# Five seven-product pairs in the second round of a feed-forward network, and later transposes into attention, on one Trainium2 core

## The chip, the core and the metric

The kernel runs on one core of one Trainium2 chip. A core has a matrix engine (TensorE, PE in the profile), a vector engine (VectorE, DVE), a scalar engine (ScalarE, ACT), GpSimd (POOL) and a queue engine (SyncE, SP) that issues most transfers. Each engine works through its own list of instructions in order and waits for semaphores of the others. PE reads its operands from SBUF and writes sums into eight banks of PSUM of 128 x 512 float32; DVE and ACT read them out.

The metric is device time in microseconds (us). A comparison of two kernels on this program can tell about 0.2% (2.6 us) from no change.

## The reference

One sequence of 512 tokens of width 1024 goes through two layers: a Mamba-2 mixer and a feed-forward network, then latent attention and a second feed-forward network, each with a residual and a layer norm behind it. What the change touches is this part:

```python
def conv_ffn(h, up, conv_w, conv_b, down):
    u = causal_depthwise_conv(h @ up, conv_w, conv_b)     # 1024 -> 2 x 2816, 3 taps
    g, val = jnp.split(u, 2, axis=-1)
    return (jax.nn.silu(g) * val) @ down                  # 2816 -> 1024
...
        h = layer_norm(DN_ALPHA * h + mix, ln_mix_g[i], ln_mix_b[i])
        ff = conv_ffn(h, ffn_up[i], ffn_conv_w[i], ffn_conv_b[i], ffn_down[i])
        h = layer_norm(DN_ALPHA * h + ff, ln_ffn_g[i], ln_ffn_b[i])
```

Behind the first feed-forward network, attention begins with two products on `h`: `h @ q_down` (384 columns) and `h @ kv_down_proj` (320 columns).

## The kernel before

Every float32 operand is split into a high part (the value rounded to PE's format) and the low remainder, and a product is three matmuls: high x high, high x low, low x high. Weights pass through `WStream`: SP loads a tile of 128 x 1024 into `wst`, ACT casts it to `wh` (line 96), DVE subtracts to get `wl` (line 97). Six `wh`/`wl` pairs exist, so ACT and DVE can prepare the weights of an item only when an earlier one has been used up.

A feed-forward network has 22 channel tiles (`HT`) of 128 hidden channels. For each one PE makes 48 matmuls (`mm_a`, line 159; gate and value), and `conv3_silu_gate` makes the convolution and the gating on ACT and DVE. The hidden tiles go into the down projection in two ways:

- In pairs (`down_pairs`). A pair of channel tiles, two halves of the tokens and two halves of the output columns form a product of 2 x 2 blocks, which is made with seven block products in place of eight. Each of the seven (a11, s1, s2, s4, s3, a12, a22) is made for two token tiles, by three matmuls of 512 columns for each pair; its operands are sums made on DVE (`pair_operands`), and the sums of weights are made by DMA accumulation and by DVE. The results go into the residual `h` from three sets of banks X, Y, Z (`add`, line 387).
- Directly (`piece`). For token tile i and column half hf, one bank sums the remaining channel tiles; `add_mix` (line 185) adds it into `h` with the row sum for the layer norm.

There are two rounds: round r makes its channel tiles, then its pairs. `RP0` and `RP1` give the numbers of pairs for the first and the second layer: `((2, 2, 1), (2, 1, 1))` is five pairs, in weight items of two, two and one, in the first round, and four pairs in the second. So ten channel tiles go into the first round, eight into pairs of the second, and four are left for the direct way. All hidden operands lie in 18 tiles (`gt`), given out in turn.

The end of the first network is where most of the argument lies. For each token tile i in order: two pieces, two `add_mix`, then the layer norm: `ln_mean` (line 189, DVE), `ln_squares` (194, ACT), `ln_var` (203 and 204, two operations on 128 x 1 that GpSimd makes, the second a power), `ln_a` twice (210, DVE, from `h` and the parameters `lng` into `xn`), `ln_b` twice (215, DVE, into `h`). Then `transpose_h(i)`: PE transposes the eight blocks of the tile (line 274, four into each of two banks), and ACT and DVE split each bank into the halves high and low of `ht` (277, 278). Attention's first step `down(i)` (in `mla`) needs `ht` of tile i: 48 matmuls in 16 entries on six weight items `dw`; behind it a normalisation makes `ctok`, which `down_t(i)` transposes. Before the change, tiles 0 and 1 are transposed within the network, tile 2 behind `down(0)` and tile 3 behind `down(1)`.

A scheduler decides the order on PE, DVE, ACT and GpSimd from the order in which the code issues; only SP's order is written by hand.

Of the kernel before, what the change touches and what calls it, by code (L numbers as in the profile page):

```python
# [20 lines left out]
NT = SEQ // P  # L21
DM = 1024
KT = DM // P
HID = 2816
HT = HID // P
# [259 lines left out]

RP0 = ((2, 2, 1), (2, 1, 1))
RP1 = ((2, 2, 1), (2, 1, 1))


def rounds(rp):
    r0 = 2 * sum(rp[0])
    return r0, r0 + 2 * sum(rp[1])


def ffn_items(up, down, rp):

    it = []
    R0, R1 = rounds(rp)
    dv = down.rearrange("(k p) n -> p k n", p=P)
    for r, ks in enumerate((range(R0), range(R0, HT))):
        for c in ks:
            it.append((up[c], 1024))
            it.append((up[c + HT], 1024))

        for odd, hf, kinds in ((0, 0, "r"), (0, 1, "a"), (1, 1, "+="), (0, 0, "-"), (1, 0, None), (1, 0, "a")):
            j = ks[0]  # L310
            for p, n in enumerate(rp[r]):
                b = dv[:, j:j + 2 * n, hf * 512:(hf + 1) * 512].rearrange("p (k e) n -> p k e n", e=2)[:, :, odd, :]
                it += [(b, n * 512, kind, p) for kind in kinds or (None,)]
                j += 2 * n
    for hf in range(2):
        for j in range(R1, HT, 2):
            it.append((dv[:, j:j + 2, hf * 512:(hf + 1) * 512], 1024))
    return it
# [39 lines left out]
    split(k, s34, v)  # L358


def down_pairs(k, ws, n, prs, parts, first, between):

    nc = k.nc
    X, Y, Z = ([k.bank() for _ in range(2)] for _ in range(3))
    ni = len(parts)
    at = [sum(parts[:p]) for p in range(ni + 1)]
    new = {(i, hf) for i in range(NT) for hf in range(2)} if first else set()  # L370

    def product(bs, op, p, i, start, stop):
        wh, wl = ws.get(i, 3)
        ps = prs[at[p]:at[p + 1]]
        for t in range(2):
            for q, pr in enumerate(ps):
                x, c0 = pr[op]
                sl = slice(q * 512, (q + 1) * 512)
                k.mm_b(bs[t], x, slice(c0 + t * P, c0 + (t + 1) * P), wh[:, sl], wl[:, sl],
                       start and p == 0 and q == 0, stop and p == ni - 1 and q == len(ps) - 1)  # L380
        ws.retire(i)

    def add(bs, row, hf, sign):
        for t in range(2):
            i = 2 * row + t
            hs = k.h[:, i, hf * 512:(hf + 1) * 512]
            last = nc.vector.scalar_tensor_tensor(hs, hs, ALPHA if (i, hf) in new else 1.0, bs[t], op0=ALU.mult,  # L387
                                                  op1=ALU.add if sign > 0 else ALU.subtract)
            new.discard((i, hf))
        return last  # L390

    def ahead(n, ins):

        with k.tc.issue_after(ins.ins):
            ws.ahead(n)

    for p in range(ni):
        product(X, "a11", p, n + p, True, True)
    n += ni
    ahead(n, add(X, 0, 0, 1))  # L400
    for p in range(ni):
        product(Y, "s1", p, n + p, True, True)
    n += ni
    ahead(n, add(Y, 1, 1, 1))
    between()
    for p in range(ni):
        product(X, "s2", p, n + 2 * p, False, True)
        product(Y, "s4", p, n + 2 * p + 1, False, True)
    n += 2 * ni
    add(X, 0, 1, -1)  # L410
    ahead(n, add(Y, 0, 1, 1))
    for bs, op, s0, out in ((X, "s3", False, (1, 1, -1)), (Z, "a12", True, (0, 0, 1)), (X, "a22", False, (1, 0, 1))):
        for p in range(ni):
            product(bs, op, p, n + p, s0, True)
        n += ni
        ahead(n, add(bs, *out))
    return n


def ffn(k, ws, base, cwp, gb, rp, la=2, out=None, mid=None):  # L420

    nc, tc = k.nc, k.tc
    R0, R1 = rounds(rp)
    with ExitStack() as c:
        pool = lambda n, b: c.enter_context(tc.tile_pool(name=n, bufs=b))
        pools = {"gt": pool("gt", 18), "fw": pool("fw", 7), "rs": pool("rs", 1), "cw": pool("cw", 1)}
        k.junk = (pools["fw"], "acc")
        cw = pools["cw"].tile([P, 2 * HT, 4], F32, name="cw")
        nc.sync.dma_start(cw, cwp)
        n = base  # L430
# [3 lines left out]
        rs = k.lnp.tile([P, 2, DM], F32, name="rs", tag="lngb")  # L434
        ws.sums = [rs[:, 0], rs[:, 1], pools["rs"].tile([P, 512], F32, name="rs2")]
        new_gt = lambda: pools["gt"].tile([P, 2, SEQ], F32R, name="gt")
# [8 lines left out]
        for r in range(2):  # L445
            gts, prs = [], []

            half = [new_gt().rearrange("p x (e t) -> p e x t", e=2) for _ in range((sum(rp[r]) + 1) // 2)]
            even = []

            def finish(ci, bg, bv):
                if ci >= R1:
                    gts.append(new_gt())
                    conv3_silu_gate(k, pools, bg, bv, cw, ci, gts[-1])
                    return
                av = conv3_silu_gate(k, pools, bg, bv, cw, ci, None)
                if ci % 2 == 0:
                    even.append(av)
                    return
                j = len(prs)  # L460
                a11, a2, s12, s34 = half[j // 2][:, j % 2], new_gt(), new_gt(), new_gt()
                pair_operands(k, pools, even.pop(), av, a11, a2, s12, s34)
                prs.append({"a11": (a11, 0), "a12": (a2, 0), "a22": (a2, 256), "s1": (s12, 0), "s2": (s12, 256),
                            "s3": (s34, 0), "s4": (s34, 256)})

            c0 = r * R0
            if k.pend:

                nh = 2 + len(k.pend)
                bs = [k.bank() for _ in range(4)]  # L470
                wv = lambda i, la=None: [x.rearrange("p (k m) -> p k m", k=KT) for x in ws.get(n + i, la)]
                for i in range(nh - 1):
                    k.mm_a(bs[i][:, :256], wv(i, nh - 2 - i), k.ht, slice(0, 256))
                k.flush()
                with tc.issue_after(k.ln_end.ins), tc.issue_after(k.ln_sq.ins):
                    ws.ahead(n + nh - 1, 0)
                    ws.ahead(n + 5, 0)
                k.mm_a(bs[nh - 1][:, :256], wv(nh - 1, 0), k.ht, slice(0, 256))
                for i in range(4):
                    c = 256 if i < nh else 0  # L480
                    k.mm_a(bs[i][:, c:], wv(i, 0), k.ht, slice(c, 512))
                    ws.retire(n + i)
                    if i % 2:
                        ws.ahead(n + i + 1)
                        finish(c0 + i // 2, bs[i - 1], bs[i])
                n += 4
                c0 += 2
            for ci in range(c0, HT if r else R0):
                bg, bv = k.bank(), k.bank()
                ws.ahead(n + 1)  # L490
                for b, i in ((bg, n), (bv, n + 1)):
                    w = [x.rearrange("p (k m) -> p k m", k=KT) for x in ws.get(i)]
                    k.mm_a(b, w, k.ht, slice(0, 512))
                    ws.retire(i)
                n += 2
                ws.ahead(n)
                finish(ci, bg, bv)
            if mid and not r:
                mid()
            n = down_pairs(k, ws, n, prs, rp[r], not r, norm_params if r else lambda: None)  # L500
        if out is None:
            k.new_ht()

# [21 lines left out]
        for i in range(NT):  # L525
            last = i == NT - 1
            b = k.bank()
# [14 lines left out]
            b = k.bank()  # L542
# [1 line left out]
            if last:  # L544
                ws.ahead(n + 2 * nw, la)
            k.add_mix(i, 1, b, 1.0, True)
            if out is None and i >= 2:
                k.transpose_h(i - 2)
            xn[i] = row("xn")
            k.ln_stats(i)  # L550
            if out is None:
# [7 lines left out]
        n += 2 * nw  # L559
    ws.nst = 3  # L560
    if out is None:
        k.pend = [lambda: k.transpose_h(NT - 2), lambda: k.transpose_h(NT - 1)]
    return n

NH, HD, NG, HPG, NS = 32, 64, 8, 4, 128
# [6 lines left out]

LAG = [15, 15, 7.6, 5, 7.6, 13]
DRAM = bass.MemoryType.DRAM


def ssd_items(xbc, zdt, zw, ow):
# [540 lines left out]
def mla(k, ws, base, ngp, gb):  # L1118
    nc, tc = k.nc, k.tc
    with ExitStack() as cx:  # L1120
# [16 lines left out]
        n = [base]  # L1137
        tok = {}

        def down(i):  # L1140
            bq, bk = k.bank(), k.bank()
            ts = slice(i * P, (i + 1) * P)
            plan = []
# [6 lines left out]
                plan.append((j, bq[:, :QR], 5 + 2 * (j - 4), QR, QR))  # L1150
            seen = set()
            for c, (j, o, kk, off, w) in enumerate(plan):
                wh, wl = ws.get(n[0] + j)
                last = o.shape[1] == QR and kk == 7 or o.shape[1] != QR and kk == 7
                k.mm_b(o, ht[kk], ts, wh[:, off:off + w], wl[:, off:off + w], kk == 0, last)
                if i == NT - 1 and (c == len(plan) - 1 or plan[c + 1][0] != j):
                    ws.retire(n[0] + j)
# [54 lines left out]
            rope(k, qr[:, i].rearrange("p (h d) -> p h d", h=AH), b.rearrange("p (h d) -> p h d", h=AH), i, AH, tmp, nc.gpsimd)  # L1212

        for i in range(NT):
            down(i)
            if k.pend:
                k.pend.pop(0)()
            if i:
                down_t(i - 1)
        H = {}  # L1220
# [231 lines left out]
```

## Time and profile before

| | |
|---|---|
| time, median of 3 runs (range) | 1312.17 us (1312.11 to 1312.66) |
| the profiled execution's own time | 1312.25 us |
| its span, first to last instruction | 1310.5 us |
| PE busy | 1300.4 us, 99% of the span |
| DVE busy | 1014.7 us, 77% |
| ACT busy | 635.0 us, 48% |
| POOL busy | 93.6 us, 7% |
| share of PE in the chain that ended last | 94% |

The first network's second round of pairs and its direct pieces lie between about 674 and 772 us of the span, and attention's first step begins at 772.60. The 1.75 us between the span and the time lie outside the instructions and are taken as fixed.

### The profile page before, as it was taken

Reading aid. Unit: us, or ns where it says so; the run is one execution under the profiler, and the core shown is the slowest. Engines: PE = TensorE matmul, PEld = TensorE weight load, DVE = VectorE, ACT = ScalarE, POOL = GpSimd, SP = SyncE. Lnnn points to the kernel's source line nnn. Section 1 sums busy time; section 2 is a strip of 40 time slices with the busy share of each in tenths; the row PEclk is TensorE's granted clock in tenths of the full one; section 3 lists DMA queues with packets and bytes.
Section 4 is the critical chain, followed back from the end, with each engine's and each line's share of the span. In section 5 each row is a group of like instructions: output and inputs, shape, how many; then the busy total and the mean of one; then the engine's idle time right before and its main releaser. Section 6 shows DMA issues by size and latency. Waiting matters only on the chain.

```text
span 1310.5 us, 17403 instructions
## 1 busy us (share of the span) xinstructions
PE 1300.4 (99%) x6666; PEld 1098.0 (84%) x6666; DVE 1014.7 (77%) x1581; ACT 635.0 (48%) x1029; POOL 93.6 (7%) x96
## 2 busy tenths in 40 slices
PE   9999999999999999999999999999999999999997
PEld 8888888888888988888888899888898888888886
DVE  7688898787798868866776876998587686667587
ACT  5765555456353644444443434665254444444341
POOL 0111011011011001100000012000100010000000
PEclk9999999999999999999999999999999999999999
DMA  8423314313420533352322721320143227322251
GB/s 297 179 113 113 121 41 145 129 44 135 167 73 1 179 129 82 71 204 98 125 65 33 247 88 61 104 90 33 35 149 136 77 35 215 129 97 105 41 161 65
DMA packets 49780, 144.59 MB, mean 110 GB/s; under 512 B 5313, under 2 KB 6337, under 8 KB 48417
## 3 DMA queue, kind: packets, MB, share of 16 engines
q1 hardware_dynamic: 44480, 133.57, 29.0%
q0 software_dynamic: 5072, 9.77, 4.4%
q8 instruction: 52, 0.85, 0.3%
q14 instruction: 32, 0.25, 0.1%
q10 hardware_dynamic: 144, 0.15, 0.0%
HBM read 141.30 MB, written 2.16 MB: 109 GB/s over the span
## 4 chain that ended last, share of the span: by engine, by line
PE 94%; DVE 4%; ACT 1%; issue 1%; DMA 0%; SPq 0%; DVEq 0%; ACTq 0%
PE ps L159 56%; PE ps L165 10%; PE ps L167 10%; PE ps L166 10%; PE ps L801 1%; PE ps L809 1%; DVE wl L97 1%; PE ps L274 1%; PE ps L790 1%; PE ps L1260 1%; PE ps L768 1%; PE ps L912 1%; PE ps L742 1%; DVE PT L1286 0%; ACT E L1272 0%
## 5 line engine op out<-in xcount | busy, mean ns | idle before, releaser
L159 PE MATMUL ps<-ht,wh 128*128 128x512 f32 (+1 forms) x2256 | 517.8, 380 | 0.0
L159 PEld LDWEIGHTS ps<-ht,wh 128*128 128x128 f32 x2256 | 407.8, 188 | 79.4 <-issue 0.7
L97 DVE TENSOR_TENSOR wl<-wst,wh 128x1024 fp32r<-128x1024 f32 (+3 forms) x222 | 254.1, 1159 | 40.0 <-ACT wh L96 37.6
L96 ACT CAST wh<-wst 128x1024 fp32r<-128x1024 f32 (+3 forms) x222 | 218.9, 996 | 107.8 <-PE ps L167 53.8
L159 PE MATMUL ps<-ht,wl 128*128 128x512 f32 (+1 forms) x1128 | 266.8, 379 | 0.0
L159 PEld LDWEIGHTS ps<-ht,wl 128*128 128x128 f32 x1128 | 205.1, 188 | 39.8
L328 DVE SCALAR_TENSOR_TENSOR acc<-ps,cw,acc 128x511 f32<-128x511 f32 x88 | 65.7, 747 | 80.0 <-ACT acc L327 80.0
L165 PE MATMUL ps<-wh,gt 128*128 128x512 f32 (+1 forms) x320 | 123.7, 387 | 0.0
L167 PE MATMUL ps<-wh,gt 128*128 128x512 f32 (+1 forms) x320 | 123.6, 386 | 0.0
L166 PE MATMUL ps<-wl,gt 128*128 128x512 f32 (+1 forms) x320 | 123.6, 386 | 0.0
L657 DVE SCALAR_TENSOR_TENSOR cv<-ps,cw,cv 128x511 f32<-128x511 f32 (+2 forms) x96 | 71.2, 745 | 34.1 <-ACT cv L655 33.5
L340 ACT CAST gt<-acc 128x512 fp32r<-128x512 f32 (+1 forms) x80 | 44.0, 571 | 102.0 <-DVE acc L333 99.4
L327 ACT ACTIVATE acc<-ps,cw 128x512 f32<-128x512 f32 x88 | 68.2, 775 | 29.4 <-PE ps L159 29.3
L167 PEld LDWEIGHTS ps<-wh,gt 128*128 128x128 f32 x320 | 60.1, 188 | 12.2
L332 ACT ACTIVATE acc<-acc 128x512 f32<-128x512 f32 x44 | 27.8, 633 | 87.7 <-DVE acc L329 87.6
L166 PEld LDWEIGHTS ps<-wl,gt 128*128 128x128 f32 x320 | 60.1, 188 | 12.2
L165 PEld LDWEIGHTS ps<-wh,gt 128*128 128x128 f32 x320 | 60.1, 188 | 12.1
L329 DVE SCALAR_TENSOR_TENSOR acc<-ps,cw,acc 128x510 f32<-128x510 f32 x88 | 65.8, 748 | 2.5
L52 POOL DMA_DIRECT2D rs<-in_down_dram x24 | 25.4, 1057 | 572.7 <-DVE wl L97 572.7
L96 ACT CAST wh<-rs 128x1024 fp32r<-128x1024 f32 (+1 forms) x48 | 39.9, 835 | 45.7 <-DVE rs L88 27.2
L341 DVE TENSOR_TENSOR gt<-acc,gt 128x512 fp32r<-128x512 f32 (+1 forms) x80 | 48.8, 627 | 13.5 <-ACT gt L340 13.5
L387 DVE SCALAR_TENSOR_TENSOR h<-h,ps 128x512 f32<-128x512 f32 x56 | 37.6, 686 | 25.3 <-PE ps L167 25.3
(242 smaller groups left out, 1744.7 us busy)
## 6 DMA issues: line engine op xcount, KB each, us to landing
wst<-in_up_dram SPq DMA_DIRECT2D x88, 512.0 KB, 3.5
wst<-in_xbc_dram SPq DMA_DIRECT2D x32, 512.0 KB, 5.9
wst<-in_down_dram SPq DMA_DIRECT2D x26, 512.0 KB, 5.4
W<-cumd SPq DMA_DIRECT2D x8, 1024.0 KB, 4.6
wst<-in_sow_dram SPq DMA_DIRECT2D x16, 512.0 KB, 4.6
wst<-in_zw_dram SPq DMA_DIRECT2D x14, 512.0 KB, 6.4
rs<-in_down_dram POOLq DMA_DIRECT2D x12, 512.0 KB, 6.8
wst<-in_down_dram SPq DMA_DIRECT2D x18, 256.0 KB, 2.6
```

Of the source, the lines that this page charges most:

```text
L96: nc.scalar.copy(h[:, :f], s[:, :f])
L97: nc.vector.tensor_tensor(l[:, :f], s[:, :f], h[:, :f], op=ALU.subtract)
L159: nc.tensor.matmul(out, w[:, k, :], xts[k][:, x, ts], start=first and p == 0 and k == 0, stop=last and p == 2 and k == nk - 1, skip_group_ ...
L165: nc.tensor.matmul(out, xt[:, 0, tsl], wh, start=start, stop=False, skip_group_check=True)
L166: nc.tensor.matmul(out, xt[:, 0, tsl], wl, start=False, stop=False, skip_group_check=True)
L167: nc.tensor.matmul(out, xt[:, 1, tsl], wh, start=False, stop=stop, skip_group_check=True)
L327: nc.scalar.activation(a, b, AF.Identity, bias=cw[:, ch, 3:4], scale=cw[:, ch, 2:3])
L328: nc.vector.scalar_tensor_tensor(a[:, 1:], b[:, :SEQ - 1], cw[:, ch, 1:2], a[:, 1:], op0=ALU.mult, op1=ALU.add)
L329: nc.vector.scalar_tensor_tensor(a[:, 2:], b[:, :SEQ - 2], cw[:, ch, 0:1], a[:, 2:], op0=ALU.mult, op1=ALU.add)
L340: k.nc.scalar.copy(dst[:, 0, :], src)
L341: k.nc.vector.tensor_tensor(dst[:, 1, :], src, dst[:, 0, :], op=ALU.subtract)
L657: nc.vector.scalar_tensor_tensor(t[:, d:], b[:, :SEQ - d], cw[:, ch, 3 - d:4 - d], t[:, d:], op0=ALU.mult, op1=ALU.add)
```

## The change

The first layer's second round takes five pairs in place of four, so only two channel tiles (20 and 21) are left for the direct way. With five pairs, all 18 `gt` tiles are in use, so these two channel tiles are computed late: behind the product a11, which frees its operand tiles (`late`, `RL`). The banks Y and Z are taken later, the layer norm's parameters are loaded behind the products s2 and s4, and a pair's operand tiles are given out in another order. In the second layer the numbers of pairs stay, and `RL` is 22, so nothing comes late. At the end of the first network only tile 0 is transposed there; the transposes of tiles 1, 2 and 3 are issued inside `down(0)`, `down(1)` and `down(2)`, before the entry `MID` (11 of 16).

```diff
-RP0 = ((2, 2, 1), (2, 1, 1))
+RP0 = ((2, 2, 1), (2, 2, 1))
 RP1 = ((2, 2, 1), (2, 1, 1))
...
+NGT = 18
...
     r0 = 2 * sum(rp[0])
-    return r0, r0 + 2 * sum(rp[1])
+    r1 = r0 + 2 * sum(rp[1])
+    return r0, r1, min(HT, r1 + NGT - 3 * sum(rp[1]) - (sum(rp[1]) + 1) // 2)
...
+    ups = lambda cs: [(up[c + e], 1024) for c in cs for e in (0, HT)]
+    for r, ks in enumerate((range(R0), range(R0, RL))):
+        it += ups(ks)
...
+            if r and kinds == "r":
+                it += ups(range(RL, HT))
...
-def down_pairs(k, ws, n, prs, parts, first, between):
+def down_pairs(k, ws, n, prs, parts, first, late, between):
...
-    X, Y, Z = ([k.bank() for _ in range(2)] for _ in range(3))
+    new_banks = lambda: [k.bank() for _ in range(2)]
+    X = new_banks()
...
     ahead(n, add(X, 0, 0, 1))
+    n = late(n)
+    Y = new_banks()
     for p in range(ni):
         product(Y, "s1", p, n + p, True, True)
     n += ni
     ahead(n, add(Y, 1, 1, 1))
-    between()
...
     n += 2 * ni
+    between()
+    Z = new_banks()
...
-                a11, a2, s12, s34 = half[j // 2][:, j % 2], new_gt(), new_gt(), new_gt()
+                a11, s12, s34, a2 = half[j // 2][:, j % 2], new_gt(), new_gt(), new_gt()
...
+            n = channels(range(c0, RL if r else R0), n)
             if mid and not r:
                 mid()
+            late = lambda n: channels(range(RL, HT), n) if r else n
+            n = down_pairs(k, ws, n, prs, rp[r], not r, late, norm_params if r else lambda: None)
...
-            if out is None and i >= 2:
-                k.transpose_h(i - 2)
+            if out is None and i == 2:
+                k.transpose_h(0)
...
-        k.pend = [lambda: k.transpose_h(NT - 2), lambda: k.transpose_h(NT - 1)]
+        k.pend = [lambda i=i: k.transpose_h(i) for i in range(1, NT)]
...
+MID = 11
...
             for c, (j, o, kk, off, w) in enumerate(plan):
+                if mid and c == MID:
+                    mid()
...
         for i in range(NT):
-            down(i)
-            if k.pend:
-                k.pend.pop(0)()
+            down(i, k.pend.pop(0) if k.pend else None)
             if i:
                 down_t(i - 1)
```

What the scheduler makes of this shows in the order of the instructions. The names are those of the build, and the numbers behind them count buffers and differ between the two builds; `ps` is a PSUM bank.

First, PE behind the product a11 of the second round (bank `ps_6021`), as changed: the late channel tiles stand there, and the next product s1 (bank `ps_6215`) stands behind them.

```order
L167 MATMUL ps_6021<-wh_5916,gt_5214 128x512
L159 MATMUL ps_6070<-ht_3696,wh_5933 128x512 x8
L159 MATMUL ps_6070<-ht_3696,wl_5934 128x512 x8
L159 MATMUL ps_6070<-ht_3696,wh_5933 128x512 x8
L159 MATMUL ps_6071<-ht_3696,wh_5987 128x512 x8
```

Before the change these matmuls stand ahead of the round's products.

Second, PE at the border of the network and attention. Before: the last piece (`ps_6620`, tile 3), the transposes of tile 1 (`ps_6658` and `ps_6665`), then `down(0)` (`ps_6706`, `ps_6707`).

```order
L167 MATMUL ps_6620<-wh_6455,gt_6141 128x512
L274 MATMUL ps_6658<-ident_86,h_93 128x128 x4
L274 MATMUL ps_6665<-ident_86,h_93 128x128 x4
L165 MATMUL ps_6706<-wh_6461,ht_6467 128x384
L166 MATMUL ps_6706<-wl_6462,ht_6467 128x384
L167 MATMUL ps_6706<-wh_6461,ht_6467 128x384
```

The same place as changed: `ps_6632` is the last piece, `ps_6721` and `ps_6728` take the transposes of tile 1, `ps_6686` and `ps_6687` belong to `down(0)`.

```order
L167 MATMUL ps_6632<-wh_6465,gt_6202 128x512
L165 MATMUL ps_6686<-wh_6495,ht_6521 128x384
L166 MATMUL ps_6686<-wl_6496,ht_6521 128x384
L165 MATMUL ps_6687<-wh_6495,ht_6521 128x320
L166 MATMUL ps_6687<-wl_6496,ht_6521 128x320
L274 MATMUL ps_6721<-ident_86,h_93 128x128 x4
L274 MATMUL ps_6728<-ident_86,h_93 128x128 x4
L167 MATMUL ps_6686<-wh_6495,ht_6521 128x384
```

The scheduler has moved the transposes of tile 1 up: four matmuls of `down(0)` stand ahead of them. The transposes of tile 0 keep their place, behind the pieces of tiles 0, 1 and 2 and ahead of those of tile 3.

Third, DVE at the first direct pieces. Before: three subtractions of coming weights, the two additions of tile 0, its mean, and at once `ln_a`.

```order
L97 TENSOR_TENSOR wl_6456<-wst_6333,wh_6455 128x1024
L97 TENSOR_TENSOR wl_6462<-wst_6339,wh_6461 128x1024
L97 TENSOR_TENSOR wl_6476<-wst_6363,wh_6475 128x1024
L185 SCALAR_TENSOR_TENSOR h_93,lnst_6487<-h_93,ps_6468 128x512
L185 SCALAR_TENSOR_TENSOR h_93,lnst_6487<-h_93,ps_6489 128x512
L189 TENSOR_SCALAR lnst_6487<-lnst_6487 128x1
L210 SCALAR_TENSOR_TENSOR xn_6503<-h_93,lnst_6487,lng_6243 128x512 x2
L185 SCALAR_TENSOR_TENSOR h_93,lnst_6524<-h_93,ps_6511 128x512
L215 SCALAR_TENSOR_TENSOR h_93<-xn_6503,lnst_6487,lnb_6244 128x512 x2
```

As changed, the third subtraction stands between the two additions, and both additions of tile 1 (`lnst_6560`) stand ahead of tile 0's `ln_a`.

```order
L97 TENSOR_TENSOR wl_6510<-wst_6369,wh_6509 128x1024
L97 TENSOR_TENSOR wl_6516<-wst_6375,wh_6515 128x1024
L185 SCALAR_TENSOR_TENSOR h_93,lnst_6529<-h_93,ps_6522 128x512
L97 TENSOR_TENSOR wl_6533<-wst_6405,wh_6532 128x1024
L185 SCALAR_TENSOR_TENSOR h_93,lnst_6529<-h_93,ps_6531 128x512
L185 SCALAR_TENSOR_TENSOR h_93,lnst_6560<-h_93,ps_6553 128x512
L189 TENSOR_SCALAR lnst_6529<-lnst_6529 128x1
L185 SCALAR_TENSOR_TENSOR h_93,lnst_6560<-h_93,ps_6564 128x512
L210 SCALAR_TENSOR_TENSOR xn_6545<-h_93,lnst_6529,lng_6355 128x512 x2
L215 SCALAR_TENSOR_TENSOR h_93<-xn_6545,lnst_6529,lnb_6356 128x512 x2
```

For the tiles 1 and 2 it is alike: an addition of the next tile stands between the mean and `ln_a`. The two splits of tile 0's transposes (line 278) stand behind the layer norm of tile 1 and the second addition of tile 2.

## Rows read from the trace of the kernel before

**Rows 1.** The page: busy time, share and instructions by engine; the chain that ended last.
```profile
PE 1300.4 (99%) x6666; PEld 1098.0 (84%) x6666; DVE 1014.7 (77%) x1581; ACT 635.0 (48%) x1029; POOL 93.6 (7%) x96
...
PE 94%; DVE 4%; ACT 1%; issue 1%; DMA 0%; SPq 0%; DVEq 0%; ACTq 0%
```

**Rows 2.** Waits of TensorE (PE), whole span: us in total, times, longest us.
```profile
PE ps L620 <- DVE warm L135: 1.1, 1, 1.1
PE ps L1260 <- DVE qrT L1248: 0.7, 2, 0.4
PE ps L1260 <- DVE kT L1232: 0.6, 1, 0.6
```

**Rows 3.** Stretches: us, busy us by engine, granted TensorE clock, DMA share, GB/s.
```profile
532.00:580.00 48.00, 48.00 (x213) 39.77 (x212) 37.25 (x47) 21.55 (x26) 3.28 (x3) 1.00 0.48 140
674.00:749.00 75.00, 75.00 (x333) 62.10 (x332) 53.91 (x72) 33.31 (x46) 5.95 (x6) 1.00 0.41 115
749.00:773.00 24.00, 24.00 (x116) 20.10 (x115) 20.98 (x38) 9.59 (x15) 2.67 (x6) 1.00 0.29 97
```

**Rows 4.** Timeline of PE in a channel product: start us, us, line, shape, count.
```profile
449.50 3.79 PE L159 MATMUL ps<-ht,wh 128*128 128x512 f32 x16
...
454.94 3.79 PE L159 MATMUL ps<-ht,wh 128*128 128x512 f32 x16
```

**Rows 5.** Timeline of PE where the first feed-forward network ends.
```profile
765.48 1.03 PE L274 MATMUL ps<-ident,h 128*128 128x128 f32 x8
766.26 0.48 PE L165 MATMUL ps<-wh,gt 128*128 128x512 f32 x1
...
771.81 1.04 PE L274 MATMUL ps<-ident,h 128*128 128x128 f32 x8
772.60 0.42 PE L165 MATMUL ps<-wh,ht 128*128 128x384 f32 x1
...
780.38 1.03 PE L274 MATMUL ps<-ident,h 128*128 128x128 f32 x8
```

**Rows 6.** Timeline of VectorE (DVE) in the same place.
```profile
749.96 3.49 DVE L97 TENSOR_TENSOR wl<-wst,wh 128x1024 fp32r<-128x1024 f32 x3
753.36 0.68 DVE L185 SCALAR_TENSOR_TENSOR h<-h,ps 128x512 f32<-128x512 f32 x1
...
754.79 0.69 DVE L185 SCALAR_TENSOR_TENSOR h<-h,ps 128x512 f32<-128x512 f32 x1 [0.74 <-PE ps L167]
...
755.52 0.21 DVE L189 TENSOR_SCALAR lnst<-lnst 128x1 f32<-128x1 f32 x1
755.77 1.42 DVE L210 SCALAR_TENSOR_TENSOR xn<-h,lnst,lng 128x512 f32<-128x512 f32 x2
757.51 0.69 DVE L185 SCALAR_TENSOR_TENSOR h<-h,ps 128x512 f32<-128x512 f32 x1 [0.33 <-PE ps L167]
...
758.12 1.41 DVE L215 SCALAR_TENSOR_TENSOR h<-xn,lnst,lnb 128x512 f32<-128x512 f32 x2
...
767.32 1.28 DVE L278 TENSOR_TENSOR ht<-ps,ht 128x512 fp32r<-128x512 f32 x2
768.52 0.75 DVE L210 SCALAR_TENSOR_TENSOR xn<-h,lnst,lng 128x512 f32<-128x512 f32 x1
```

**Rows 7.** Timeline of GpSimd (POOL) in the same place.
```profile
757.17 0.18 POOL L203 TENSOR_SCALAR lnst<-lnst 128x1 f32<-128x1 f32 x1 [29.50 <-ACT lnjunk L194]
757.44 0.57 POOL L204 TENSOR_TENSOR lnst<-lnst,mhalf 128x1 f32<-128x1 f32 x1
...
768.69 0.98 POOL L204 TENSOR_TENSOR lnst<-lnst,mhalf 128x1 f32<-128x1 f32 x1
```

**Rows 8.** GpSimd and VectorE at the layer norm after the attention layer.
```profile
937.96 0.75 POOL L203 TENSOR_SCALAR lnst<-lnst 128x1 f32<-128x1 f32 x1 [6.82 <-ACT lnjunk L194]
938.79 0.95 POOL L204 TENSOR_TENSOR lnst<-lnst,mhalf 128x1 f32<-128x1 f32 x1
...
937.91 1.41 DVE L210 SCALAR_TENSOR_TENSOR h<-h,lnst,lngb 128x512 f32<-128x512 f32 x2 [0.34 <-ACT lnjunk L194]
```

More of the change, by code (lines that the diff above doesn't have):

```diff
@@ L284, in flush @@
         self.pend = []
-RP0 = ((2, 2, 1), (2, 1, 1))
+RP0 = ((2, 2, 1), (2, 2, 1))
 RP1 = ((2, 2, 1), (2, 1, 1))
+NGT = 18
 def rounds(rp):
     r0 = 2 * sum(rp[0])
-    return r0, r0 + 2 * sum(rp[1])
+    r1 = r0 + 2 * sum(rp[1])
+    return r0, r1, min(HT, r1 + NGT - 3 * sum(rp[1]) - (sum(rp[1]) + 1) // 2)
 def ffn_items(up, down, rp):
     it = []
-    R0, R1 = rounds(rp)
+    R0, R1, RL = rounds(rp)
     dv = down.rearrange("(k p) n -> p k n", p=P)
[L304 to L307, printed above, removed]
+    ups = lambda cs: [(up[c + e], 1024) for c in cs for e in (0, HT)]
+    for r, ks in enumerate((range(R0), range(R0, RL))):
+        it += ups(ks)
         for odd, hf, kinds in ((0, 0, "r"), (0, 1, "a"), (1, 1, "+="), (0, 0, "-"), (1, 0, None), (1, 0, "a")):
@@ L422, in ffn @@
     nc, tc = k.nc, k.tc
-    R0, R1 = rounds(rp)
+    R0, R1, RL = rounds(rp)
     with ExitStack() as c:
         pool = lambda n, b: c.enter_context(tc.tile_pool(name=n, bufs=b))
-        pools = {"gt": pool("gt", 18), "fw": pool("fw", 7), "rs": pool("rs", 1), "cw": pool("cw", 1)}
+        pools = {"gt": pool("gt", NGT), "fw": pool("fw", 7), "rs": pool("rs", 1), "cw": pool("cw", 1)}
         k.junk = (pools["fw"], "acc")
@@ L487, in ffn, with channels @@
                 c0 += 2
[L488 to L497, printed above, removed]
+            def channels(cs, n):
+                for ci in cs:
+                    bg, bv = k.bank(), k.bank()
+                    ws.ahead(n + 1)
+                    for b, i in ((bg, n), (bv, n + 1)):
+                        w = [x.rearrange("p (k m) -> p k m", k=KT) for x in ws.get(i)]
+                        k.mm_a(b, w, k.ht, slice(0, 512))
+                        ws.retire(i)
+                    n += 2
+                    ws.ahead(n)
+                    finish(ci, bg, bv)
+                return n
+            n = channels(range(c0, RL if r else R0), n)
             if mid and not r:
                 mid()
-            n = down_pairs(k, ws, n, prs, rp[r], not r, norm_params if r else lambda: None)
+            late = lambda n: channels(range(RL, HT), n) if r else n
+            n = down_pairs(k, ws, n, prs, rp[r], not r, late, norm_params if r else lambda: None)
         if out is None:
@@ L1138, in mla, with down @@
         tok = {}
-        def down(i):
+        def down(i, mid):
             bq, bk = k.bank(), k.bank()
```

## The prediction

> **What bounds the kernel now.** I read the page first: PE is busy 99% of the span and 94% of the chain that ended last is PE [rows 1]. Then the list of PE's waits, which has three rows: 1.1 us at the start, and 0.7 and 0.6 us in attention [rows 2]; nothing in the feed-forward networks appears there. Then the stretches: in round 0's five-pair products (532 to 580), around the second round's products (674 to 749) and at the network's end (749 to 773) PE is busy for the whole of each stretch, at a granted clock of 1.00, which is the 2.4 GHz level [rows 3]. So a matmul that goes away is worth its own slot, and any wait that PE gets is added in full. The reader should also see how near DVE is to that limit: 20.98 us of 24.00 at the network's end, against 53.91 of 75.00 ahead of it [rows 3]. That is the only stretch here in which a second engine is nearly full, and the change shortens PE's part of it.
>
> **What is removed.** A pair costs 7 products x 2 token tiles x 3 = 42 matmuls; two channel tiles in the direct way cost 2 x 4 x 2 x 3 = 48. One more pair saves 6 matmuls. Two starts 24 matmuls apart are 5.44 us apart [rows 4], so one slot is 0.2267 us, and the gain is **6 x 0.2267 = 1.36 us**, 0.10% of the time. Nothing larger is in the change: the 96 matmuls of the late channel tiles only move.
>
> **What the moves cost in the products.** The fifth pair adds DVE and ACT work and larger weight items. Round 0 already has exactly this pattern (five pairs in items of two, two and one) and PE is busy 48.00 of 48.00 us there, with DVE at 37.25 [rows 3]; so I cost it at nothing, under PE's own 48 us. The late channel tiles stand between a11 and s1. Their two last convolutions would hold s1 back only if DVE were behind, and their 21.8 us (96 slots) need fewer DVE operations than an early channel pair, whose pair operands are left out. The operand tiles of the late channels are those of a11, read just before them, and their first write comes only after 48 slots (10.9 us). The loads of `lng` and `lnb` stand on SP's queue ahead of the last three full `dw` loads and two shorter ones; they wait for the products a11 and s2, which are long done then. I take 0 for all of it; the bound from above is one late item, two slots of SP and one subtraction, some 1 us by the 1.13 us between the subtractions of 1024 (three from 749.96 to 753.36) [rows 6].
>
> **Where the time goes instead: the network's end.** The pieces shrink from 12 slots (2.72 us) to 6 (1.36 us), 96 matmuls to 48, or 10.9 us less for PE. DVE's work in the same place stays: eight additions, four layer norms, the splits, six weights of attention. I follow it from t = 0 at the start of the pieces. In the kernel before, that is 765.48 less 72 slots (16.32) = 749.16 [rows 5]. DVE ends the additions of the last product at t = 0.80 (the next operation starts at 749.96) [rows 6], the same as after the change.
>
> Tile 0, in the new order of DVE: two subtractions of 1.13 (to 3.07), an addition of 0.61 (3.68), a subtraction (4.81), the second addition (5.42), tile 1's addition (6.03), the mean of tile 0. No piece is late for these: piece k is there at 1.36 k + 0.2. From the mean's start to the first `ln_b` it takes 2.60 us (755.52 to 758.12), through ACT's squares and GpSimd's two operations [rows 6, 7]. That gives 8.63, if GpSimd is undisturbed. It will not be: before, the two `ln_a` follow the mean at once and end at 757.19, as GpSimd begins at 757.17; now an addition stands between, the second `ln_a` runs from 7.46 to 8.20, and GpSimd begins at 6.03 + 1.65 = 7.68. Where an `ln_a` ran, GpSimd's first operation took 0.75 instead of 0.18 [rows 7, 8], and ended as that `ln_a` did; the power took 0.98 and 0.95 instead of 0.57. Here the first is held until 8.2, the power comes behind it undisturbed: about +0.3. So `ln_b` runs from 8.93, its halves end at 9.68 and 10.34. PE stands before the transposes of tile 0 at 6 x 1.36 = 8.16. It waits for the first half until about 9.78 (**1.62 us**; 0.1 from DVE's end to PE), makes four transposes (0.44), and waits for the second until 10.44 (**0.22**). They end at 10.88.
>
> Tile 1: its mean follows the `ln_b` at 10.26, and its own `ln_b` starts 2.9 later, at 13.2, and ends at 14.6; behind it comes the second addition of tile 2 (15.2). PE makes tile 3's pieces (2.72), four matmuls of `down(0)` (0.7) and stands at the transposes of tile 1 at 14.3. The first bank goes; the second has to be released by that addition of tile 2: **0.5 us**. Then `down(0)` needs the low half of tile 0, whose split on DVE stands behind that same addition: **0.2**. `down(0)` takes 7.78 us (772.60 to 780.38) [rows 5]. Its last four entries need two weights whose subtractions stand on DVE behind the layer norm of tile 2; by the same steps (mean at 16.4, `ln_b` at 19.3, to 20.6, 0.87 for 768 columns) the first is there at 21.5, and PE is there at 21.1: **0.4 to 0.5**. Last, `down_t(0)` needs `ctok` of tile 0, which DVE can only make behind all four layer norms; by the same steps about **0.6**. The transposes also stand apart in one place more: the first matmul behind a group of them took 0.32 instead of 0.23 (766.26 to 766.58), **0.1**.
>
> **The sum.** 1.62 + 0.22 + 0.5 + 0.2 + 0.45 + 0.6 + 0.1 = 3.7 us of new waits against 1.36 us saved: **+2.3 us**. Profiled time 1312.25 + 2.3 = **1314.6 us**; the profiled time is 0.08 above the runs' median of 1312.17, so it is +0.19% on that. Since PE has 94% of the chain that ended last [rows 1], I carry the shift through in full. Without GpSimd's delays (0.3 at each of the tiles 0, 1 and 2, and 0.1 for the rest) it is +1.3; with no new wait at all -1.36 + 0.1.
>
> A rule bears on the 0.3: the Trainium skill, GPSIMD Engine Reference, Specifications, says that GpSimd's SBUF interfaces are shared with VectorE, with contention where a DVE instruction has two SBUF inputs. `ln_a` is such an instruction (`h` and `lng`), the additions out of PSUM are not, and the rows agree with the rule (0.75 and 0.95 against 0.18 and 0.57). The rule speaks against this change: by it the weight subtractions and `ln_b`, which also have two SBUF inputs, would hold GpSimd too, and the sum would be that of rival 1.
>
> **The rivals.**
> 1. *All of GpSimd's operations are held.* If each of the pairs takes 0.75 + 0.95 as in rows 8 instead of 0.18 + 0.57, a layer norm's chain grows by 0.95, 0.65 more than I charge. It is paid at the transposes of tile 0, at those of tile 1 and at the late weights: +2.0, so +4.3 and **1316.5 us**, slower. For it: the new order puts an addition between the mean and `ln_a` for the tiles 0, 1 and 2. Against it: the overlap worked out here is only 0.5 us, the end of the second `ln_a`. It decides from an overlap of about 1 us.
> 2. *The gain comes through.* If DVE reaches tile 0's `ln_b` 1.9 us earlier than I say, PE finds the transposes ready and only 1.36 less 0.1 to 1.2 is kept: **1311.0 to 1312.1 us**. For it: the order before had no such wait with the same three subtractions. Against it: the pieces then gave DVE 16.3 us to the first transposes and now give 8.16, and the sum of DVE's own times to that point is 10.3.
> 3. *The late channel tiles cost.* If s1's weights or the operand tiles come late, PE waits once in each product, at most 1 us each for a few: **1317 us and more**. Against it: round 0 has the pattern without a wait [rows 3].
> 4. *The change does less than it says.* The gain is 6 slots by count and cannot fail; only faster than 1.36 us would need a wait in attention to vanish, and those are 1.3 us in all [rows 2]: 1.36 + 1.3 gives **1309.6 us**, just at the bound.
>
> **How the numbers follow.** My forecast, with 1314.0 to 1315.2 as its own range, has 0.45; its part above 1314.8 is about 0.20. (That bound is 0.2% over the runs' median, about what a measurement of this kernel can tell from no change.) Less delay by GpSimd (1312.9 to 1314.0) has 0.17, rival 2 has 0.10, rival 1 (1315.2 to 1317.2) 0.20, rival 3 0.05, and faster by over 0.2% by rival 4's last clause 0.03. Slower by over 0.2% is 0.20 + 0.20 + 0.05 = 0.45, faster 0.03, and the rest, 0.25 + 0.17 + 0.10 = 0.52, lies within. The range from 1312.0 to 1317.2 leaves out rival 3, the faster case and most of rival 2, about 0.17.
>
> **What would show it.** PE busy less than the whole of the stretch at the network's end, with a wait of 1.2 to 2 us for `ln_b` (DVE h, the line of 215) ahead of the first transposes (line 274), and one of some 0.5 us inside the second group. No wait of PE between the late channel tiles and s1. 6 matmuls fewer. GpSimd's first operation at 0.4 to 0.6 in the first tiles, not 0.18. I am wrong if the first transposes start without a wait, or if PE waits in the second round's products.

## The result, and the profile after

| | before | changed |
|---|---|---|
| time, median of 11 runs (range) | 1312.39 us (1311.96 to 1312.68) | 1315.53 us (1315.29 to 1316.80) |
| the profiled execution's own time | 1312.25 us | 1315.65 us |
| its span | 1310.5 us | 1313.9 us |

The ratio is 1.0025, with a 95% interval of 1.0018 to 1.0033: 3.14 us more. The forecast was +2.3 us on the profiled time (1314.6 us), with a range of 1312.0 to 1317.2; the profiled time rose by 3.40 us. The measured time lies within that range, but above the narrower one, 1314.0 to 1315.2, that the prediction gave to its own account.

The page of the changed kernel, busy time by engine, answers to the first line of [rows 1]. PE has 6 matmuls fewer, as the diff says.

```profile
PE 1300.8 (99%) x6660; PEld 1096.9 (83%) x6660; DVE 1018.3 (78%) x1585; ACT 637.8 (49%) x1029; POOL 94.9 (7%) x96
```

The last two stretches of [rows 3] in the changed kernel, and one more behind them. The columns are those of [rows 3].

```profile
674.00:749.00 75.00, 75.00 (x333) 62.12 (x332) 55.94 (x72) 33.37 (x44) 4.24 (x4) 1.00 0.46 123
749.00:773.00 24.00, 22.59 (x105) 18.39 (x104) 17.95 (x31) 9.94 (x14) 1.88 (x4) 1.00 0.35 110
773.00:796.00 23.00, 21.59 (x137) 20.19 (x136) 17.56 (x42) 8.34 (x20) 5.01 (x11) 1.00 0.15 44
```

The second round's products are as full as before: 75.00 of 75.00, at the same clock. PE stands for 1.41 us in the stretch where the network ends, and for 1.41 us in the next. In the kernel before PE is busy for the whole of that one too, as a longer stretch from the same start shows:

```profile
773.00:807.00 34.00, 34.00 (x224) 33.87 (x223) 20.73 (x48) 13.81 (x34) 5.44 (x13) 1.00 0.22 71
```

PE's waits in the changed kernel; those of [rows 2] are still there and are left out here.

```profile
PE ps L274 <- DVE h L215: 1.4, 1, 1.4
...
PE ps L1202 <- PE ps L167: 0.6, 1, 0.6
PE ps L1202 <- DVE ctok L1194: 0.3, 1, 0.3
PE ps L274 <- DVE h L185: 0.3, 1, 0.3
PE ps L166 <- DVE wl L97: 0.2, 1, 0.2
```

These are the four places that the forecast named. Line 274 waits twice: for the first `ln_b` (line 215), and in the transposes of tile 1 for the second addition of tile 2 (line 185). Line 166 waits for the late weights. Line 1202 is the transpose of `ctok` in `down_t(0)`. Its first row names PE itself, which had long been done, so the releaser has to be looked for elsewhere.

The list rounds, and it counts only the time in which PE's modelled end has passed. The exact loss is read from starts. PE's timeline of the changed kernel at the four places:

```profile
766.79 0.39 PE L167 MATMUL ps<-wh,gt 128*128 128x512 f32 x1
768.59 1.32 PE L274 MATMUL ps<-ident,h 128*128 128x128 f32 x8 [1.41 <-DVE h L215]
769.66 0.48 PE L165 MATMUL ps<-wh,gt 128*128 128x512 f32 x1
...
773.14 0.60 PE L274 MATMUL ps<-ident,h 128*128 128x128 f32 x4
774.04 0.66 PE L274 MATMUL ps<-ident,h 128*128 128x128 f32 x4 [0.30 <-DVE h L185]
774.65 0.59 PE L167 MATMUL ps<-wh,ht 128*128 128x384 f32 x2
...
779.72 0.34 PE L165 MATMUL ps<-wh,ht 128*128 128x384 f32 x1
780.29 0.45 PE L166 MATMUL ps<-wl,ht 128*128 128x384 f32 x1 [0.24 <-DVE wl L97]
780.58 0.34 PE L167 MATMUL ps<-wh,ht 128*128 128x384 f32 x1
780.75 0.33 PE L165 MATMUL ps<-wh,ht 128*128 128x384 f32 x1
...
790.76 0.34 PE L167 MATMUL ps<-wh,ht 128*128 128x384 f32 x1
791.65 0.79 PE L1202 MATMUL ps<-ident,ctok 128*128 128x128 f32 x5 [0.55 <-PE ps L167]
...
793.28 0.33 PE L1202 MATMUL ps<-ident,ctok 128*128 128x128 f32 x1 [0.32 <-DVE ctok L1194]
793.36 0.39 PE L165 MATMUL ps<-wh,ht 128*128 128x320 f32 x1
```

- Tile 0: the last piece ahead of the transposes has its slot until 766.79 + 0.23 = 767.02, and the transposes start at 768.59: 1.57 us. From their start to the next product they take 1.07 us, where they took 0.78 before [rows 5]: 0.29. Together **1.86 us** (forecast 1.62 + 0.22).
- Tile 1: 1.51 us from the transposes' start to 774.65, against 0.79 before [rows 5]: **0.72 us** (forecast 0.5 + 0.2).
- The late weights: 0.57 and 0.29 us between starts, where the same width takes 0.17 (780.58 to 780.75): **0.52 us** (forecast 0.45).
- `ctok`: 2.60 us from 790.76 to 793.36. Experiment 1 has the same matmuls without a wait in 1.35 us, so it is **1.25 us** (forecast 0.6).

That is 4.35 us; less the 1.36 us saved it is +2.99. The measured +3.14 leaves 0.15 us, of which the forecast put 0.1 down to the regrouping of the transposes; it was not traced further.

Since the differences are small, I also use a ruler finer than the times: the stretch from the first transposes ahead of the first feed-forward network to the first transposes behind attention's layer norm. It holds all that the change touches. PE's timeline of the kernel before has its two ends here:

```profile
413.83 1.03 PE L274 MATMUL ps<-ident,h 128*128 128x128 f32 x8
...
935.02 1.04 PE L274 MATMUL ps<-ident,h 128*128 128x128 f32 x8
```

and that of the changed kernel here:

```profile
414.02 1.03 PE L274 MATMUL ps<-ident,h 128*128 128x128 f32 x8
...
938.35 0.82 PE L274 MATMUL ps<-ident,h 128*128 128x128 f32 x6
```

The last row counts six of the eight transposes, since its view ends at 939; only the start is used. It is 521.19 us before and 524.33 us after: +3.14. The start of this stretch lay between 413.83 and 414.65 in the profiles of this study, though the code ahead of it is the same in all of them; spans carry that difference, the stretch does not.

The last of the four waits is the one that came out twice as large as forecast. The chain that ended last, in order of time, says what released it:

```profile
785.07 1.43 DVE h L215 x2
...
787.08 3.73 DMA ang<-in_ang_dram
...
790.93 0.62 DVE ctok L1189
```

`ang` is the parameter row of attention's normalisation (640 values for each partition). It is loaded through GpSimd's queue into a tile with the tag `E3`, which lies in a pool that opens behind the network. GpSimd issues the load only when the last `ln_b` (line 215) has ended. With it on the path, `ctok` starts at 790.93. In the kernel before, the same load was issued at 781.52, behind PE's transposes of tile 2, and DVE waited for it too (1.28 us, until 785.07). PE was still busy with `down(1)` then: it reached `down_t(0)` at 789.83, 3.1 us behind the start of the last operation on `ctok` (786.70). I had not followed this load.

### The profile page after: what moved, and what is told of

Same layout as the page of the kernel before. It is cut to its first block, busy times and chain, and to the rows that moved or that the text cites. A ratio compares the mean times of both kernels' runs of the same rounds, so it can differ in the third digit from the quotient of the medians.

```text
span 1313.9 us, 17388 instructions
## 1 busy us (share of the span) xinstructions
PE 1300.8 (99%) x6660; PEld 1096.9 (83%) x6660; DVE 1018.3 (78%) x1585; ACT 637.8 (49%) x1029; POOL 94.9 (7%) x96
## 5 line engine op out<-in xcount | busy, mean ns | idle before, releaser
L97 DVE TENSOR_TENSOR wl<-wst,wh 128x1024 fp32r<-128x1024 f32 (+4 forms) x220 | 253.4, 1165 | 39.4 <-ACT wh L96 38.0
L96 ACT CAST wh<-wst 128x1024 fp32r<-128x1024 f32 (+4 forms) x220 | 218.0, 1001 | 109.2 <-PE ps L167 62.6
```

Of the source, the lines that this page charges most:

```text
L96: nc.scalar.copy(h[:, :f], s[:, :f])
L97: nc.vector.tensor_tensor(l[:, :f], s[:, :f], h[:, :f], op=ALU.subtract)
```

## The experiments

All kernels were timed in 11 runs beside the kernel before, whose median was 1312.41 us beside experiments 1 to 4 and 1312.66 us beside 5 to 8. "Stretch" is the ruler above, from each kernel's own profile, less the 521.19 us of the kernel before.

| | median, us (range) | ratio to before, 95% | stretch, us |
|---|---|---|---|
| the change | 1315.53 (1315.29 to 1316.80) | 1.0025, 1.0018 to 1.0033 | +3.14 |
| 1 `ang` early | 1314.44 (1314.11 to 1314.62) | 1.0014, 1.0005 to 1.0023 | +1.74 |
| 2 weights later | 1313.63 (1313.21 to 1315.01) | 1.0009, 1.0000 to 1.0018 | +1.13 |
| 3 pairs only | 1315.29 (1314.78 to 1316.16) | 1.0021, 1.0012 to 1.0030 | +2.94 |
| 4 moves only | 1312.75 (1312.13 to 1313.51) | 1.0001, 0.9992 to 1.0010 | +0.03 |
| 5 both 1 and 2 | 1312.45 (1311.45 to 1314.06) | 0.9999, 0.9990 to 1.0008 | -0.40 |
| 6 late tiles only | 1313.04 (1312.28 to 1313.49) | 1.0001, 0.9992 to 1.0010 | +0.25 |
| 7 filler in experiment 1 | 1314.33 (1313.70 to 1314.60) | 1.0010, 1.0001 to 1.0019 | +1.70 |
| 8 filler in the kernel before | 1313.72 (1313.48 to 1315.44) | 1.0009, 1.0000 to 1.0017 | +1.34 |

**1. `ang` early.** The changed kernel, with `ang` in a tile of the layer norms' own pool, so that the load need not wait for the network's end.

```diff
-        ng = one.tile([P, QR + KVR], F32, name="ang", tag="E3")
+        ng = k.lnp.tile([P, QR + KVR], F32, name="ang", tag="lngb")
```

> The changed kernel, with the normalisation parameters of attention (ang) in a tile that is free earlier, so that their load need not wait for the last layer norm. Theory: the loss is the sum of PE's waits at the border of network and attention, and the last of them (0.72 and 0.49 us more than a matmul's slot ahead of the transposes of ctok) comes from this load, which lands at 790.8 us, right ahead of the first ctok operation. Then these waits go, the others stay, and the time falls by about 1.2 us, to 1314.3. Rival, the step of the prediction: ctok is late because DVE makes it behind four layer norms; then the wait stays at 0.6 us or more and the time falls by at most 0.6.

It took 1.1 us off the time and 1.40 us off the stretch, and both waits of line 1202 are gone from the list. GpSimd issues the load at 748.76, 38 us earlier. PE's timeline at `down_t(0)`:

```profile
790.77 0.34 PE L167 MATMUL ps<-wh,ht 128*128 128x384 f32 x1
790.94 0.82 PE L1202 MATMUL ps<-ident,ctok 128*128 128x128 f32 x6
...
792.12 0.31 PE L165 MATMUL ps<-wh,ht 128*128 128x320 f32 x1
```

The six transposes follow at once, and the next product is reached 1.35 us behind 790.77. On DVE, `ctok` now waits for GpSimd's power, not for the load:

```profile
788.64 0.62 DVE L1189 SCALAR_TENSOR_TENSOR ctok<-ps,css,ang 128x384 f32<-128x384 f32 x1 [2.12 <-POOL css L1188]
```

So the forecast's reason for this term, DVE's order behind four layer norms, costs nothing by itself: `ctok` still stands behind all four, and no wait is left. The load is the cause; the last layer norm matters in the changed kernel because the load starts behind it. The edit moves both its tile and its place in GpSimd's list, so which of the two had held it was not separated.

**2. Weights later.** The changed kernel, with the preparation of the weights of the pieces and of attention issued later in the code: behind the last product's additions and behind each `ln_a`.

```diff
-        ahead(n, add(bs, *out))
+        if bs is X and op == "a22" and not first and tail is not None:
+            with k.tc.issue_after(add(bs, *out).ins):
+                ws.ahead(n, tail)
+        else:
+            ahead(n, add(bs, *out))
...
-                wh, wl = ws.get(n + hf * nw + jc)
+                wh, wl = ws.get(n + hf * nw + jc, 0 if out is None else None)
...
+            if out is None and (1, 2, 3, None)[i] is not None:
+                ws.ahead(n + 2 * nw, (1, 2, 3, None)[i])
```

> The changed kernel, with two of attention's weight subtractions taken out of DVE's queue ahead of the first two additions and put behind the first ln_a. Theory: two subtractions are 2.27 us, the wait of PE ahead of the transposes of tile 0 (2.0 us in all) falls to 0.1 to 0.4 us, the later ones stay, and the time falls by 1.6 to 2.0 us, to about 1313.7. Rival: the wait is made by GpSimd or by the chain of the layer norm itself, whatever stands ahead of it; then the wait stays over 1 us and the time within 0.7 us of the changed kernel.

It took 1.9 us off the time and 2.01 us off the stretch. Both waits of line 274 left the list. But the scheduler did not do what the code and the expectation say: no subtraction of 1024 went behind an `ln_a`. DVE in the changed kernel, from the last product's additions (line 395) on:

```profile
758.38 1.37 DVE L395 SCALAR_TENSOR_TENSOR h<-h,ps 128x512 f32<-128x512 f32 x2 [2.02 <-PE ps L167]
759.66 2.36 DVE L97 TENSOR_TENSOR wl<-wst,wh 128x1024 fp32r<-128x1024 f32 x2
...
762.54 1.22 DVE L97 TENSOR_TENSOR wl<-wst,wh 128x1024 fp32r<-128x1024 f32 x1
```

and in experiment 2:

```profile
758.54 0.69 DVE L395 SCALAR_TENSOR_TENSOR h<-h,ps 128x512 f32<-128x512 f32 x1 [0.89 <-PE ps L167]
759.14 1.22 DVE L97 TENSOR_TENSOR wl<-wst,wh 128x1024 fp32r<-128x1024 f32 x1
760.28 0.68 DVE L395 SCALAR_TENSOR_TENSOR h<-h,ps 128x512 f32<-128x512 f32 x1
...
761.48 1.22 DVE L97 TENSOR_TENSOR wl<-wst,wh 128x1024 fp32r<-128x1024 f32 x1
...
766.43 1.41 DVE L215 SCALAR_TENSOR_TENSOR h<-xn,lnst,lnb 128x512 f32<-128x512 f32 x2 [0.25 <-POOL lnst L204]
```

Of the three subtractions behind the additions of the last product, one has moved up into DVE's idle time ahead of them (2.02 us, now 0.89; four subtractions stand there in a row, where three did), one stands between them, and one between the additions of tile 0 as before. The pieces start at 759.03 here. The mean of tile 0 starts 4.88 us behind that, where it was 6.03: one subtraction less. Now `ln_a` follows the mean at once and is nearly over when GpSimd begins, and GpSimd's first operation takes 0.18 us, not 0.55: from the mean to `ln_b` it is 2.52 us, where it was 2.89. So `ln_b` starts at 7.40, where it was 8.92. The expected time came out, but not by the two subtractions (2.27 us) behind `ln_a` that it rested on; that part was luck. PE's timeline at the transposes of tile 0:

```profile
766.96 0.39 PE L167 MATMUL ps<-wh,gt 128*128 128x512 f32 x1
767.24 1.32 PE L274 MATMUL ps<-ident,h 128*128 128x128 f32 x8
768.32 0.48 PE L165 MATMUL ps<-wh,gt 128*128 128x512 f32 x1
```

The slot of the last piece ends at 767.19 and the transposes start 0.05 us behind it, where it was 1.57. The 0.30 us inside them (1.08 against 0.78) stay: the second half of `ln_b` is still only just behind. So what tile 0's `ln_b` waits for is DVE's own list of subtractions and additions (1.15 us of the 1.52) and GpSimd's first operation (0.37), as the forecast said. The wait for `ctok` did not shrink (791.47 less 788.77 is 2.70 us here); it hangs on the load, which comes behind the last `ln_b`.

**3 and 4. The two halves of the change.** Experiment 3 keeps five pairs and the late channel tiles and puts the transposes back as they were; experiment 4 keeps the transposes' new places and the new order of banks and loads, and goes back to four pairs.

```diff
-            if out is None and i == 2:
-                k.transpose_h(0)
+            if out is None and i >= 2:
+                k.transpose_h(i - 2)
...
-            down(i, k.pend.pop(0) if k.pend else None)
+            down(i, None)
+            if k.pend:
+                k.pend.pop(0)()
```

```diff
-RP0 = ((2, 2, 1), (2, 2, 1))
+RP0 = ((2, 2, 1), (2, 1, 1))
```

> Five pairs and the late channel tiles, with the transposes where they were before the change. Theory: the shorter pieces make the loss, so the waits at the transposes of tile 0 (2.0 us) and tile 1 (about 0.7) are there too, and the time is 1.5 to 3 us over that of before, 1314 to 1315.4. Rival: the moved transposes make the loss; then the waits are gone and the time is 1.3 us under that of before, 1311.1.

> Four pairs as before, with the other parts of the change (transposes in attention, later banks and parameters, the other order of operand tiles); no channel tile is late. Theory: with pieces of 12 matmuls DVE keeps up, PE has no wait at the border, and the time is that of before within 0.4 us. Rival: the moved transposes make the loss, 2 to 3 us over the time of before.

Experiment 3 keeps nearly the whole loss (+2.94 of +3.14), and experiment 4 none of it. The moved transposes cost 0.2 us at most and save nothing; what is left, with experiment 6 below, is the fifth pair with its shorter pieces. In experiment 3 the list of PE's waits reads much the same: 1.4 us for `ln_b`, 0.2 for the late weights, and 0.3 and 0.4 at line 1202; the transposes of tile 1 start 0.28 us late there.

**5. Both cures.** Experiments 1 and 2 together; DVE's order is that of experiment 2, so again no subtraction of 1024 stands behind an `ln_a`.

> The changed kernel with both mends: attention's parameters loaded early, and two of its weight subtractions behind the first ln_a. Theory: of 4.7 us of waits at the border, 2.9 to 3.2 go; what stays (the second bank of tile 1's transposes or the low half of tile 0, and the two late weights) is 0.8 to 1.8 us, about what the six matmuls give: 0.5 us under to 0.4 us over the time of before. Rival: the waits hang together and are only pushed on; then it stays over 1.5 us above the time of before.

The loss is gone, and the time ties with the kernel before. On the stretch it is 0.40 us shorter. What is left of the waits: 0.3 inside the transposes of tile 0 (1.07 us for 0.78), 0.5 for the late weights, 0.1 for a regrouping; less the 1.36 saved that makes -0.46. So the 6 matmuls are worth what the count says once nothing waits, and even then it is 0.03% of the time. No version here beats the kernel before by a measurable amount.

**6. Late tiles only.** The change's code with four pairs, but channel tiles 20 and 21 still computed behind a11; tiles 18 and 19 stay early.

```diff
-RP0 = ((2, 2, 1), (2, 2, 1))
+RP0 = ((2, 2, 1), (2, 1, 1), 20)
...
-    return r0, r1, min(HT, r1 + NGT - 3 * sum(rp[1]) - (sum(rp[1]) + 1) // 2)
+    return r0, r1, rp[2] if len(rp) > 2 else min(HT, r1 + NGT - 3 * sum(rp[1]) - (sum(rp[1]) + 1) // 2)
```

> Four pairs as before in the second round, with the last two channel tiles computed behind its first product, and the rest of the change. Theory: the late channel tiles cost nothing, PE does not wait in the second round nor at the border, and the time is that of before within 0.4 us. Rival: the late place costs a part of the loss (s1 waits for its weights or the operand tiles); then PE waits between the late matmuls and s1 and the time is 1 us or more over that of before.

It ties with the kernel before; the 0.25 us on its stretch lie in attention, where the wait for `qrT` is 1.0 us and not 0.7 [rows 2]. The stretch of the products:

```profile
674.00:749.00 75.00, 75.00 (x332) 62.13 (x331) 53.87 (x71) 33.94 (x46) 3.85 (x4) 1.00 0.39 113
```

PE is full there. Rival 3 is refuted, here and in the changed kernel itself.

**7 and 8. The same 6 matmuls in two kernels.** Six matmuls of 128 x 512 whose bank is never read stand ahead of the transposes of tile 0, in experiment 1's kernel and in the kernel before. They add work to what the reference needs.

```diff
+            wh0, wl0 = ws.get(n)
...
+                fb = k.bank()
+                for _ in range(2):
+                    k.mm_b(fb, gts[0], slice(i * P, (i + 1) * P), wh0[:, :512], wl0[:, :512], True, True)
```

> The kernel of the early parameters with six matmuls more (of a kind with the pieces, into a bank that nobody reads) ahead of the transposes of tile 0: 1.36 us of work that adds nothing to the result. Theory: PE stands idle there for 1.6 us, so they cost nothing: the time is that of the kernel of the early parameters within 0.3 us, and the wait there shrinks to some 0.2 us. Rival: PE's work sets the time there; then it is 1.36 us more.

> The kernel before with the same six matmuls more at the same place, whose results nobody reads. Theory: PE never idles there, so they cost their slots, 6 x 0.2267 = 1.36 us: 1313.7. It is also the measure of what the six matmuls that the change saves are worth. Rival: the matmuls at the border are hidden; then the time is that of before.

In the changed kernel they are free: 1314.33 us against 1314.44 without them. PE's timeline there:

```profile
768.44 0.39 PE L167 MATMUL ps<-wh,gt 128*128 128x512 f32 x1
768.87 1.32 PE L274 MATMUL ps<-ident,h 128*128 128x128 f32 x8
```

The wait for `ln_b` has shrunk from 1.57 us to 768.87 - 768.67 = 0.20 us, by 1.37 us, and the transposes start where they did. In the kernel before the same matmuls cost 1.1 us of the time and 1.34 us of the stretch, where 6 slots are 1.36. So a matmul slot is worth its full price in the old order, and nothing at the new place.

## Why the prediction held, and where it was off

The direction and the mechanism at the network's end were right, one term (`ctok`) had the wrong reason and half its size, and the time lay within the stated range. It did not lie within 1314.0 to 1315.2, the part of the range that the forecast kept for its own account: 1315.53 us (1315.65 profiled) lies where it had put rival 1. By the time alone one would have picked the wrong account; the rows below are what separates them. The excess over 0.2% is also small: the median is at 0.25%, and the interval begins at 0.18%.

**The gain (6 slots, 1.36 us): right.** Experiment 8 measures 1.34 on the stretch, and experiment 5 shows it come through.

**The moves in the products (0): right.** The first piece starts 36 slots (8.16 us) ahead of 767.02, at 758.86 us. Before it was 749.16, and 42 slots more are 9.52, which gives 758.68. The 0.18 us that are left were there at 414 us already (413.83 and 414.02). Nothing was lost in the products at all; experiment 6 shows the same.

**The end of the network, tiles 0 and 1: right, step by step, but for one reason.** DVE in the changed kernel:

```profile
765.62 1.42 DVE L210 SCALAR_TENSOR_TENSOR xn<-h,lnst,lng 128x512 f32<-128x512 f32 x2
767.78 1.41 DVE L215 SCALAR_TENSOR_TENSOR h<-xn,lnst,lnb 128x512 f32<-128x512 f32 x2 [0.74 <-POOL lnst L204]
...
771.97 1.41 DVE L215 SCALAR_TENSOR_TENSOR h<-xn,lnst,lnb 128x512 f32<-128x512 f32 x2 [0.72 <-POOL lnst L204]
773.30 0.68 DVE L185 SCALAR_TENSOR_TENSOR h<-h,ps 128x512 f32<-128x512 f32 x1
...
777.95 1.42 DVE L215 SCALAR_TENSOR_TENSOR h<-xn,lnst,lnb 128x512 f32<-128x512 f32 x2 [0.71 <-POOL lnst L204]
```

With t = 0 at 758.86, the first `ln_b` starts at 8.92 (forecast 8.93), that of tile 1 at 13.11 (13.2), and that of tile 2 at 19.09 (19.3). The first transposes start at 9.73 (9.78), and PE stands at those of tile 1 at 14.28 (14.3).

**GpSimd's delay (0.3 at a tile): right at tiles 0 and 2, right by luck at tile 1, and rival 1 fell.** GpSimd in the changed kernel:

```profile
766.54 0.55 POOL L203 TENSOR_SCALAR lnst<-lnst 128x1 f32<-128x1 f32 x1 [36.34 <-ACT lnjunk L194]
767.18 0.57 POOL L204 TENSOR_TENSOR lnst<-lnst,mhalf 128x1 f32<-128x1 f32 x1
771.09 0.21 POOL L203 TENSOR_SCALAR lnst<-lnst 128x1 f32<-128x1 f32 x1 [3.35 <-ACT lnjunk L194]
771.38 0.55 POOL L204 TENSOR_TENSOR lnst<-lnst,mhalf 128x1 f32<-128x1 f32 x1
776.74 0.56 POOL L203 TENSOR_SCALAR lnst<-lnst 128x1 f32<-128x1 f32 x1 [4.80 <-ACT lnjunk L194]
```

In tile 0 the first operation took 0.55 us (forecast 0.52, from 7.68 to 8.2) and ended 0.05 us behind `ln_a` (767.09 and 767.04). The power behind it took 0.57, undisturbed, not 0.95. In tile 1 GpSimd was hardly held (0.21 us; the prediction had named 0.4 to 0.6 in the first tiles as a sign). The 0.3 us came from ACT: its squares started 0.65 us behind the mean (769.76 and 769.11), not 0.31 as in tile 0 (765.20 and 764.89), since the split of tile 0's first bank (line 277, at 769.28) stood ahead of them. In both tiles the operation ended with `ln_a`, so the time came out alike.

Rival 1 wanted both operations held in each layer norm; none of the powers was. That does not speak against the rule behind it: DVE stood idle while the powers ran (0.74, 0.72 and 0.71 us ahead of `ln_b`), and neither a weight subtraction nor `ln_b` ran beside GpSimd in these layer norms. What they would do to it stays untested.

**Rival 2 (the gain comes through): fell,** since the first transposes waited 1.57 us. Experiment 5 shows what it takes: `ln_b` 1.5 us earlier, and the load out of the way as well.

**Rival 4: fell.** The waits in attention, 0.7 and 0.6 us, are in the list of the changed kernel as they were [rows 2]. The forecast carried the shift through in full, and that held: the stretch grew by 3.14 us, the median by 3.14 us.

**The late weights: right** (0.52 for 0.45).

**The term that was off: `ctok`.** The step said that "`down_t(0)` needs `ctok` of tile 0, which DVE can only make behind all four layer norms; by the same steps about 0.6". DVE's order is as it said, but four layer norms on DVE alone would not have made PE wait: with the load out of the way no wait is left (experiment 1). The load of `ang` stands behind the last `ln_b` and takes 3.73 us, and that makes 1.25 us. I had followed the weights through DVE and left out the parameter load on GpSimd's queue, which the kernel before hides behind `down(1)`. This term is 0.65 us too small, most of the 0.8 us that the forecast (+2.3) lacks of the measured +3.1 on the stretch.

## What to carry to other kernels

Where PE is the bound, taking away matmuls moves the next engine up: at the network's end DVE had 20.98 us of work in 24.00, and 10.9 us of PE's pieces were taken from beside it. Follow the engine that is nearly full through the stretch with the new due times; the terms found that way agreed within 0.1 us. Look also for its idle time just ahead: here one subtraction moved into 2.02 us of it, with GpSimd's delay that went with it, took 2.01 us off the stretch. Check in the trace what an edit did to the order before its result is read; experiment 2 did something else than its text. Then list every transfer that starts at the same border, parameter rows too, and ask for each what releases it and what hides it now: a load of 3.73 us that PE had never waited for took back 1.25 of the 1.36 us that the six matmuls saved.

## What the hardware showed

GpSimd's operation on 128 x 1 values took 0.18 us where it started 0.02 us ahead of the end of `ln_a` (757.17 and 757.19) [rows 7], and a like one (line 1186, at 787.80 in the changed kernel) took 0.18 us with DVE idle. It took 0.55 to 0.56 us in tiles 0 and 2, where it had started 0.5 us ahead of the end of `ln_a`, a DVE operation that reads `h` and `lng`. In tile 1 it started 0.16 us ahead of that end and took 0.21. In these three it ended 0.05 to 0.06 us behind `ln_a` (767.09 and 767.04, 771.30 and 771.25, 777.30 and 777.24). That reads as if GpSimd were held until DVE's operation is over, not slowed by a share. In experiment 2 an addition out of PSUM (0.69 us) ran on DVE beside the power of tile 0, and the power kept its 0.57 us. The Trainium skill, GPSIMD Engine Reference, Specifications, says that GpSimd shares its SBUF interfaces with VectorE, with contention where a VectorE instruction has two SBUF inputs; the trace agrees, with these numbers.

A wait of PE cost a little more than its length. Behind the wait for the late weights the next start came after 0.29 us where the same width takes 0.17, so 0.12 us came on top of the 0.40. In experiment 5 it was 0.27 us at the same place. Why was not tested.
